# RWKV stage: the recurrence's 128-row output products of all chunks ahead of its 64-row chain, and the low-rank decay and rate as stacked fp32r products

## The chip, the cores and the metric

The kernel runs on one core of a Trainium2 chip. The metric is the device time of one execution in microseconds (us). TensorE is the matrix engine (PE in the rows, PEld its weight loads), DVE the vector engine, ACT the scalar engine, POOL GpSimd, SP the queue that issues the DMAs. fp32r is a 32-bit float format that TensorE multiplies in one pass and with fewer bits than fp32; a product is brought back near fp32 by splitting an operand into a high and a low part.

## The reference, cut to what matters

The program computes a first block (a hybrid of convolution and state-space layer) and a second block of two layers on 512 positions of width 1024. In the second block a layer is a feed-forward part, a mixer and another feed-forward part. The even layer's mixer joins a short convolution and an RWKV recurrence of 8 heads with 64 channels. This is the part that the change touches:

```python
r, k, v, dw, da, dg = jnp.split(p_rwkv, _RWKV_SPLITS, axis=-1)   # dw, da: 32 columns each, dg: 96
log_w = -jax.nn.softplus(-(w0 + jnp.tanh(dw) @ w_up)) - 0.5
decay = jnp.exp(-jnp.exp(log_w))
a = jax.nn.sigmoid(a0 + da @ a_up)
...
def step(S, inp):
    r_t, w_t, k_t, v_t, a_t, b_t = inp
    Sa = jnp.einsum('bhvk,bhk->bhv', S, a_t)
    S = S * w_t[:, :, None, :] + Sa[..., None] * b_t[:, :, None, :] + v_t[..., None] * k_t[:, :, None, :]
    return S, jnp.einsum('bhvk,bhk->bhv', S, r_t)
```

The output is then normalized by head, gated and projected together with the convolution's output.

## The kernel before, in words

Activations lie transposed: channels on the 128 partitions, the 512 positions along the free axis. Weights are streamed by SP's queue (`wload`, L234), split into a high part by a cast on ACT (L235) and a low part by a subtraction (L236, on POOL in this stage, on DVE elsewhere), and each 128x128 block is multiplied in three fp32r matmuls of 512 columns (L247, L248, L249). Split activations are made by a cast on ACT (L253) and a subtraction on DVE (L254).

The RWKV stage is the function `even`. Its 8 heads are worked on in two halves of four heads; a half is two pairs of heads (`jj` = 0, 1), and the two heads of a pair share the 128 partitions. The 512 positions are cut into 8 chunks of 64. For each half these steps follow each other:

- `lora` (once): the columns of dw and da come out of the input projection in a tile `la`: rows 0 to 31 for the decay, 32 to 63 for the rate. L1147 takes the Tanh of the first 32. `inproj` projects and shifts k, r and v.
- `prep_half`: decay and rate for 128 channels at a time by fp32 products with 32 rows (L1194, L1198) of `la` with the weights `wau`, then a scan of the logarithms of the decay and exponentials, on ACT, DVE and POOL.
- `quads` (L1249): products of all pairs of positions in a chunk, masked on DVE (L1253). A part goes out to memory (`nd`) and comes back in another layout, `subst` inverts small triangles on DVE, the result goes out (`td`) and comes back (`b<-td`).
- `wmats` (L1309 to L1336) completes the inverses of the 64x64 triangles by small products; `uvmats` (L1350, L1356) transposes; `premats` (L1381 to L1406) makes for each chunk a transition matrix and an added term, in two groups of four chunks (`g` = 0, 1), and the tile `u_`, whose lower 64 rows come out of this step.
- `chain_half`: for each chunk `cc` and each pair of heads the state is carried on by two products of 64 rows (L1438), an fp32 matmul being two instructions in the trace, and an addition on DVE into the next state; the chunk's output is a product of 128 rows that needs no state (L1445, 64 output channels of one head) and, from the second chunk on, one of 64 rows on the state (L1448). Both add up in a bank of PSUM for each pair of heads (`yb`). At the end ACT copies the banks out (L1457).
- `post_half` normalizes (sums by L1471 and L1475, root and reciprocal L1477 and L1478, spread by L1482) and gates (L1489); `outp` projects.

The first half's chain stands in the program after the second half's `quads` and `subst`; the convolution (`conv_in`, `conv_out`) and the first half's output are work without a place in this order. A planner in the framework sorts all instructions by the priorities of EV_PRIO and its own simulated times, engine by engine, and puts in the waits; each engine then runs its list in order. Buffers of 128x512 come from a first-in, first-out list `S` of 27; a buffer that was given back comes to the end of it. `tc.issue_after(x)` makes the instructions of its block stand behind x on their engine.

The chain's loop before:

```python
ps = yb[jj][:, 64 * cc:64 * cc + 64]
for h, sl in enumerate(hs):
    MM(ps[sl], u_[:, 128 * c4 + 64 * h:128 * c4 + 64 * h + 64], d["qt"][jj, h, g][0][:, c4, 64:128],
       start=True, stop=cc == 0)
    if cc:
        MM(ps[sl], state(jj, cc)[sl], a4[sl, cc, 1], start=False, stop=True)
```

Of the kernel before, what the change touches and what calls it, by code (L numbers as in the profile page):

```python
# [8 lines left out]
F32 = mybir.dt.float32  # L9
R = mybir.dt.float32r  # L10
AF = mybir.ActivationFunctionType
ALU = mybir.AluOpType
PSUM = bass.MemoryType.PSUM
T = 512
# [26 lines left out]
def pack(inp):  # L41
    f = {}
    a = {k: np.asarray(v) for k, v in inp.items()}
# [34 lines left out]
    mu = np.zeros((14, 128), np.float32)  # L78
    mus = a["even_mu_shift_2"][0]
    mu[:12] = mus[:1536].reshape(12, 128)  # L80
    mu[12, :64], mu[13, :96] = mus[1536:1600], mus[1600:]
    put("mu", mu.T)
    for n, src in (("w0", "rwkv_w0_2"), ("a0", "rwkv_a0_2"), ("k_k", "rwkv_k_k_2"), ("k_a", "rwkv_k_a_2"),
                   ("r_k", "rwkv_r_k_2"), ("gn_w", "rwkv_ln_w_2"), ("gn_b", "rwkv_ln_b_2")):
# [19 lines left out]
    for k in range(8):  # L104
        for g in range(2):
# [17 lines left out]
    ew = a["even_w_in_2"][0]  # L123
    wpad = np.zeros((1024, 26 * 128), np.float32)
    wpad[:, :3072] = ew[:, :3072]
    wpad[:, 3072:3136], wpad[:, 3200:3296] = ew[:, 3072:3136], ew[:, 3136:3232]
    cb, rr, kk, vv = 0, 12, 16, 20
    f["even_in"] = pairs(wpad, [(24, 25), (kk, kk + 1), (rr, rr + 1), (vv, vv + 1), (kk + 2, kk + 3),
                                (rr + 2, rr + 3), (vv + 2, vv + 3)]
                         + [(4, 8), (5, 9), (0, 1), (6, 10), (7, 11), (2, 3)])  # L130
    f["lora"] = np.concatenate([a["rwkv_w_up_2"][0], a["rwkv_a_up_2"][0]], 0)
    f["g_up"] = a["rwkv_g_up_2"][0]
    wo = a["even_w_out_2"][0].reshape(8, 128, 8, 128)

# [914 lines left out]
def even(P, nxt):  # L1049
# [8 lines left out]
    with ExitStack() as ctx:  # L1058
# [5 lines left out]
        def c(name, shape, dt=F32):  # L1064
            return ph0.tile(list(shape), dt, name=name)
# [4 lines left out]
        TS(out=half[:, 12:16], in0=half[:, 8:12], scalar1=-1.0, scalar2=1.0, op0=ALU.mult, op1=ALU.add)  # L1070
        hw0, ha0, hka, oka = (lambda j, b=b: half[:, 4 * b + j:4 * b + j + 1] for b in range(4))
        wn = c("wn", (96, 512))
        wau, nr = wn[0:64], wn[64:96]
        nc.sync.dma_start(wau, ap["lora"])
        gup = c("gup", (96, 512))
        nc.sync.dma_start(gup, ap["g_up"])
        bones = c("bones", (128, 128))
# [47 lines left out]
        def proj(i, kind="mm"):  # L1125
            h, l = P.wload(ap["even_in"][i], 2048)
            out = []
            for a in range(2):
                ps = P.bank(kind)
                P.mm3(ps, h, l, 1024 * a, P.xh, P.xl)  # L1130
                out.append(ps)
            return out
# [6 lines left out]
            STT(out=out, in0=out, scalar=P.v("mu", mi), in1=pt[:, 1:], op0=ALU.mult, op1=ALU.add)  # L1139
            return out  # L1140

        la, lg = S.get(), S.get()

        def lora():
            pa, pb = proj(0)
            shifted(pa, 12, la)
            A.activation(la[0:32], la[0:32], AF.Tanh)  # L1147
            shifted(pb, 13, lg)
            A.activation(lg, lg, AF.Tanh, scale=0.5)
            TS(out=lg, in0=lg, scalar1=0.5, scalar2=0.5, op0=ALU.mult, op1=ALU.add)  # L1150
# [22 lines left out]
        def prep_half(hf, tmp, kind):  # L1173
            d = D_[hf]
            k_, r_, v_, kkr, ar, bk, pc, bv = (d[n] for n in ("k", "r", "v", "kkr", "ar", "bk", "pc", "bv"))
            X = Slots(tmp)
            pss = P.bank(kind)
            for jj in range(2):
                j = 2 * hf + jj
                kkr[jj] = S.get()  # L1180
                TS(out=kkr[jj], in0=k_[jj], scalar1=P.v("k_k", j), scalar2=None, op0=ALU.mult)
                sq = X.get()
                A.activation(sq, kkr[jj], AF.Square)
                MM(pss[64:96], sel[:, jj, :], sq, start=jj == 0, stop=jj == 1)
                X.put(sq)
            TS(out=nr, in0=pss[64:96], scalar1=1e-24, scalar2=None, op0=ALU.max)
            A.activation(nr, nr, AF.Sqrt)
            V.reciprocal(nr, nr)

            def stages(jj):  # L1190
                j = 2 * hf + jj
                js = slice(128 * j, 128 * j + 128)
                ps = P.bank(kind)
                MM(ps, wau[0:32, js], la[0:32], start=True, stop=True)  # L1194
                ld, L = X.get(), X.get()
                A.activation(ld, ps, AF.Tanh, scale=0.5, bias=hw0(j))
                ps = P.bank(kind)
                MM(ps, wau[32:64, js], la[32:64], start=True, stop=True)  # L1198
                ta, av = X.get(), X.get()
                A.activation(ta, ps, AF.Tanh, scale=0.5, bias=ha0(j))  # L1200
                TS(out=ld, in0=ld, scalar1=1.0, scalar2=DECAY_C, op0=ALU.add, op1=ALU.mult)
                V.tensor_tensor_scan(out=L, data0=rst, data1=ld, initial=0.0, op0=ALU.mult, op1=ALU.add)
                GP.tensor_tensor(out=ld, in0=L, in1=ld, op=ALU.subtract)
                TS(out=av, in0=ta, scalar1=0.5, scalar2=0.5, op0=ALU.mult, op1=ALU.add)
                TS(out=ta, in0=ta, scalar1=hka(j), scalar2=oka(j), op0=ALU.mult, op1=ALU.add)
                yield
                e2 = X.get()
                A.activation(e2, L, AF.Exp)
                A.activation(L, L, AF.Exp, scale=-1.0)
                A.activation(ld, ld, AF.Exp)  # L1210
                e3 = L
                V.tensor_copy(pc[jj], ch(e2)[:, :, 63])
                kh = ta
                TT(out=kh, in0=ta, in1=k_[jj], op=ALU.mult)
                S.put(k_[jj])
                pk = P.bank(kind)
                MM(pk, selT[:, jj, :], nr, start=True, stop=True)
                TT(out=kkr[jj], in0=kkr[jj], in1=pk, op=ALU.mult)
                yield
                ar[jj], bk[jj] = B.get(), B.get()  # L1220
                a4, b4 = (x.rearrange("p (c a t) -> p c a t", a=2, t=64) for x in (ar[jj], bk[jj]))
                STT(out=a4[:, :, 0], in0=ch(kkr[jj]), scalar=-1.0, in1=ch(ld), op0=ALU.mult, op1=ALU.mult)
                TT(out=a4[:, :, 1], in0=ch(r_[jj]), in1=ch(e2), op=ALU.mult)
                TT(out=av, in0=av, in1=kkr[jj], op=ALU.mult)
                S.put(kkr[jj])
                TT(out=b4[:, :, 1], in0=ch(av), in1=ch(e3), op=ALU.mult)
                TT(out=b4[:, :, 0], in0=ch(kh), in1=ch(e3), op=ALU.mult)
                X.put(ld, e2, e3, av)
                yield
                STT(out=r_[jj], in0=r_[jj], scalar=P.v("r_k", j), in1=kh, op0=ALU.mult, op1=ALU.mult)  # L1230
                X.put(ta)
                pb_ = P.bank(kind)
                MM(pb_, bones, r_[jj], start=True, stop=True)
                S.put(r_[jj])
                bv[jj] = S.free.pop() if hf else S.get()
                TT(out=bv[jj], in0=pb_, in1=v_[jj], op=ALU.mult)

            return stages
# [177 lines left out]
        def chain_half(hf):  # L1416
            d = D_[hf]
            cb = P.bank("ch")
            yb = [P.bank("ch") for _ in range(2)]
            sg = [S.get() for _ in range(2)]  # L1420
            hs = [slice(64 * h, 64 * h + 64) for h in range(2)]

            def mc(jj, cc):
                m, o = d["mc"][jj, cc // 4], 64 * (cc % 4)
                return m[:, o:o + 64], m[:, 256 + o:320 + o]

            def state(jj, cc):
                return mc(jj, 0)[1] if cc == 1 else sg[jj][:, 64 * cc:64 * cc + 64]

            for cc in range(8):  # L1430
                g, c4 = cc // 4, cc % 4
                for jj in range(2):
                    if 0 < cc < 7:
                        m, c_ = mc(jj, cc)
                        s0 = state(jj, cc)
                        ps = cb[:, 256 * jj + 64 * (cc % 4):256 * jj + 64 * (cc % 4) + 64]
                        for sl in hs:
                            MM(ps[sl], m[sl], s0[sl], start=True, stop=True)  # L1438
                        TT(out=state(jj, cc + 1), in0=ps, in1=c_, op=ALU.add)
                for jj in range(2):  # L1440
                    a4 = d["ar"][jj].rearrange("p (c a t) -> p c a t", a=2, t=64)
                    u_ = d["uv"][jj, g]
                    ps = yb[jj][:, 64 * cc:64 * cc + 64]
                    for h, sl in enumerate(hs):
                        MM(ps[sl], u_[:, 128 * c4 + 64 * h:128 * c4 + 64 * h + 64], d["qt"][jj, h, g][0][:, c4, 64:128],  # L1445
                           start=True, stop=cc == 0)
                        if cc:
                            MM(ps[sl], state(jj, cc)[sl], a4[sl, cc, 1], start=False, stop=True)  # L1448
                if c4 == 3:
                    for jj in range(2):  # L1450
                        if not hf:
                            S.put(d["qt"][jj, 0, g][1], d["qt"][jj, 1, g][1])
                            if jj:
                                S.put(d["uv"][jj, g])
            for jj in range(2):
                d["yo"][jj] = S.get()
                A.copy(d["yo"][jj], yb[jj])  # L1457
                B.put(d["ar"][jj], d["wt"][jj][1])
                S.put(sg[jj])
                if not hf:  # L1460
                    S.put(d["mc"][jj, 0], d["mc"][jj, 1])
# [550 lines left out]
```

## Time and profile before

| | |
|---|---|
| median of 3 runs | 2668.18 us (2662.55 to 2675.57) |
| profiled execution | 2676.43 us, of which the span from the first to the last instruction is 2674.7 us |
| mean granted TensorE clock | 0.962 |
| the stage `even` | about 947 to 1350 us of the span |
| the two chains | 1172.5 to 1310 us of the span, woven into other work |

A span's rows tell when an engine was busy, by line of the kernel. Matmuls are pipelined, so the time that one costs is the distance from its start to the next one's, not its duration. The granted clock is given as a share of full speed.

### The profile page before, as it was taken

The numbers are of one execution on the slowest core, as the hardware profiler recorded it, in microseconds if no ns is written. First come the engines' busy times: TensorE is split into PE (matmuls) and PEld (weight loads), VectorE is DVE, ScalarE is ACT, GpSimd is POOL, SyncE is SP. The second block draws the span as 40 slices with busy tenths as digits, with TensorE's granted clock in tenths as the row PEclk, the third lists the DMA queues.
The fourth block names the chain that finished last, engine by engine and source line by source line (L and its number), as shares of the span: only waits on it lengthen the run. The fifth ranks groups of instructions, "written<-read, shape, count | busy, mean of one in ns | idle before, by whom it ended". The sixth has DMA issues, their size and how long they took to land.

```text
span 2674.7 us, 31936 instructions
## 1 busy us (share of the span) xinstructions
PE 2550.5 (95%) x12732; PEld 2075.1 (78%) x12732; DVE 1466.0 (55%) x1970; ACT 921.8 (34%) x1316; POOL 485.4 (18%) x331
## 2 busy tenths in 40 slices
PE   8687899999999999999999999999999988999999
PEld 7565788888888876778578888888888767788887
DVE  7889868455344468543564344443444776643442
ACT  5254436243223333221143223422223565422221
POOL 2499602020000164321010000100001231100000
PEclk9798999999999999898799999999999989999999
DMA  4222332323232432224122322322324422123323
GB/s 169 83 81 73 94 107 94 130 71 99 89 108 90 127 114 63 58 58 113 40 87 85 104 99 86 106 95 91 106 90 131 117 74 71 63 95 92 106 90 100
DMA packets 116230, 250.81 MB, mean 94 GB/s; under 512 B 44112, under 2 KB 53072, under 8 KB 116080
## 3 DMA queue, kind: packets, MB, share of 16 engines
q1 hardware_dynamic: 115936, 248.54, 29.7%
q8 instruction: 100, 1.64, 0.3%
q14 instruction: 50, 0.41, 0.1%
q10 hardware_dynamic: 144, 0.22, 0.0%
HBM read 234.16 MB, written 13.37 MB: 93 GB/s over the span
## 4 chain that ended last, share of the span: by engine, by line
PE 79%; DVE 9%; POOL 3%; issue 2%; ACT 2%; DMA 1%; SPq 0%; DVEq 0%; ACTq 0%; POOLq 0%
PE bank L247 24%; PE bank L248 24%; PE bank L249 23%; POOL xa L764 1%; DVE wl L236 1%; DVE xa L769 1%; PE bank L1887 1%; POOL acc L264 1%; PE bank L1445 0%; PE bank L1249 0%; DMA b<-td 0%; PE bank L1448 0%; ACT wh L235 0%; DMA s<-nd 0%; PE bank L1312 0%
## 5 line engine op out<-in xcount | busy, mean ns | idle before, releaser
L247 PE MATMUL bank<-xh,wh 128*128 128x512 f32 (+1 forms) x2152 | 841.5, 393 | 16.1 <-ACT xh L976 5.8
L235 ACT CAST wh<-raw 128x1024 fp32r<-128x1024 f32 x448 | 432.9, 967 | 1225.0 <-PE bank L248 918.0
L248 PE MATMUL bank<-xl,wh 128*128 128x512 f32 (+1 forms) x2152 | 842.3, 392 | 3.5 <-DVE xl L946 2.4
L249 PE MATMUL bank<-xh,wl 128*128 128x512 f32 (+1 forms) x2152 | 840.9, 392 | 0.2 <-DVE wl L236 0.2
L236 DVE TENSOR_TENSOR wl<-raw,wh 128x1024 fp32r<-128x1024 f32 (+2 forms) x414 | 480.5, 1161 | 327.4 <-ACT wh L235 324.8
L247 PEld LDWEIGHTS bank<-xh,wh 128*128 128x128 f32 x2152 | 409.5, 191 | 107.0 <-ACT xh L976 6.4
L248 PEld LDWEIGHTS bank<-xl,wh 128*128 128x128 f32 x2152 | 411.0, 191 | 91.7 <-DVE xl L977 4.1
L249 PEld LDWEIGHTS bank<-xh,wl 128*128 128x128 f32 x2152 | 411.0, 191 | 89.5 <-issue 5.5
L264 POOL TENSOR_TENSOR acc<-acc,sq 128x512 f32<-128x512 f32 x54 | 90.1, 1669 | 1303.9 <-ACT sq L263 1297.3
L248 PE MATMUL bank<-ml,wh 128*128 128x512 f32 x704 | 273.9, 389 | 0.0
L249 PE MATMUL bank<-mh,wl 128*128 128x512 f32 x704 | 273.9, 389 | 0.0
L247 PE MATMUL bank<-mh,wh 128*128 128x512 f32 x704 | 272.6, 389 | 0.0
L331 DVE TENSOR_TENSOR up<-bank,rs 128x512 f32<-128x512 f32 x88 | 60.8, 691 | 271.2 <-PE bank L249 271.2
L327 DVE TENSOR_TENSOR gp<-bank,rs 128x512 f32<-128x512 f32 x88 | 60.8, 691 | 174.3 <-PE bank L249 174.1
L248 PEld LDWEIGHTS bank<-ml,wh 128*128 128x128 f32 x704 | 132.2, 188 | 27.4
L247 PEld LDWEIGHTS bank<-mh,wh 128*128 128x128 f32 x704 | 132.2, 188 | 27.4
L249 PEld LDWEIGHTS bank<-mh,wl 128*128 128x128 f32 x704 | 132.2, 188 | 27.4
L236 POOL TENSOR_TENSOR wl<-raw,wh 128x1024 fp32r<-128x1024 f32 x34 | 85.5, 2515 | 176.1 <-ACT wh L235 140.6
L764 POOL TENSOR_TENSOR xa<-xa,cw 128x512 f32<-128x512 f32 x60 | 101.4, 1691 | 10.3 <-ACT cw L763 7.6
L339 DVE SCALAR_TENSOR_TENSOR xa<-bank,xa 128x512 f32<-128x512 f32 x64 | 44.3, 691 | 79.4 <-PE bank L249 79.4
L253 ACT CAST mh<-m 128x512 fp32r<-128x512 f32 x88 | 55.0, 626 | 58.7 <-DVE m L333 58.7
L742 PE MATMUL bank<-cph,wh 128*128 128x256 f32 x128 | 39.4, 308 | 32.2 <-ACT cph L725 32.2
(643 smaller groups left out, 2962.9 us busy)
## 6 DMA issues: line engine op xcount, KB each, us to landing
raw<-in_ffn_gu_dram SPq DMA_DIRECT2D x176, 512.0 KB, 3.5
raw<-in_ffn_dn_dram SPq DMA_DIRECT2D x64, 512.0 KB, 3.5
raw<-in_w_in_dram SPq DMA_DIRECT2D x46, 512.0 KB, 3.5
raw<-in_even_in_dram SPq DMA_DIRECT2D x26, 512.0 KB, 3.6
raw<-in_ffn_dn_dram SPq DMA_DIRECT2D x64, 192.0 KB, 2.3
raw<-in_conv_dram SPq DMA_DIRECT2D x16, 512.0 KB, 3.8
xa<-in_xT_dram SPq DMA_DIRECT2D x16, 256.0 KB, 4.1
raw<-in_w_co_dram SPq DMA_DIRECT2D x8, 512.0 KB, 3.4
```

Source lines behind the costliest of these rows:

```text
L235: nc.scalar.copy(h[:, :m], raw[:, :m])
L236: self.wlo.tensor_tensor(out=l[:, :m], in0=raw[:, :m], in1=h[:, :m].bitcast(F32), op=ALU.subtract)
L247: self.nc.tensor.matmul(ps, h[i][:, s], xh[k], start=a, stop=False)
L248: self.nc.tensor.matmul(ps, h[i][:, s], xl[k], start=False, stop=False)
L249: last = self.nc.tensor.matmul(ps, l[i][:, s], xh[k], start=False, stop=b)
L253: self.nc.scalar.copy(hi, src)
L264: nc.gpsimd.tensor_tensor(out=acc, in0=acc, in1=sq, op=ALU.add)
L327: nc.vector.tensor_tensor(out=gp, in0=pg, in1=rs, op=ALU.mult)
L331: nc.vector.tensor_tensor(out=up, in0=pu, in1=rs, op=ALU.mult)
L339: nc.vector.scalar_tensor_tensor(out=P.x[o], in0=ps, scalar=0.5, in1=P.x[o], op0=ALU.mult, op1=ALU.add)
L742: nc.tensor.matmul(d, h[:, o], xh, start=a, stop=False)
L764: GP.tensor_tensor(out=y, in0=y, in1=w, op=ALU.add)
```

## The change

The 128-row products of all 8 chunks are issued in a block of their own ahead of the chain, for each pair of heads and head the 8 chunks one after another; the first of each eight starts the accumulation in its half of the bank, and the others are issued behind it. The chain's loop keeps the products on the state. In `lora` the columns of dw and da are laid out twice each (rows 0 to 63 the decay's, 64 to 127 the rate's), by the packed weights; the rows of the first copy are kept as the fp32r high part, those of the second become the low part. The up-projection's weights are loaded as 128 rows (twice each), split into high and low, and a product is two fp32r matmuls of 64 rows instead of one fp32 matmul of 32. The load of these weights moves from the set-up into `lora`, and the tile `la` is given back after it.

```diff
-    mu[12, :64], mu[13, :96] = mus[1536:1600], mus[1600:]
+    mu[12], mu[13, :96] = np.concatenate([mus[1536:1568]] * 2 + [mus[1568:1600]] * 2), mus[1600:]
...
-    wpad[:, 3072:3136], wpad[:, 3200:3296] = ew[:, 3072:3136], ew[:, 3136:3232]
+    wpad[:, 3072:3200] = np.concatenate([ew[:, 3072:3104]] * 2 + [ew[:, 3104:3136]] * 2, 1)
+    wpad[:, 3200:3296] = ew[:, 3136:3232]
...
-    f["lora"] = np.concatenate([a["rwkv_w_up_2"][0], a["rwkv_a_up_2"][0]], 0)
+    f["lora"] = np.concatenate([a["rwkv_w_up_2"][0]] * 2 + [a["rwkv_a_up_2"][0]] * 2, 0)
...
-        wau, nr = wn[0:64], wn[64:96]
-        nc.sync.dma_start(wau, ap["lora"])
+        nr = wn[64:96]
+        wuh, wul, lx = c("wuh", (128, 512), R), c("wul", (128, 512), R), c("lx", (128, T), R)
...
-        la, lg = S.get(), S.get()
+        lg = S.get()
 
         def lora():
+            raw = S.get()
+            nc.sync.dma_start(raw, ap["lora"])
+            P.split(raw, wuh, wul)
+            S.put(raw)
             pa, pb = proj(0)
+            la = S.get()
             shifted(pa, 12, la)
-            A.activation(la[0:32], la[0:32], AF.Tanh)
+            A.activation(la[0:64], la[0:64], AF.Tanh)
+            A.copy(lx, la)
+            for o in (32, 96):
+                TT(out=lx[o:o + 32], in0=la[o:o + 32], in1=lx[o:o + 32].bitcast(F32), op=ALU.subtract)
+            S.put(la)
...
-                MM(ps, wau[0:32, js], la[0:32], start=True, stop=True)
+                for n, w in enumerate((wuh, wul)):
+                    MM(ps, w[0:64, js], lx[0:64], start=n == 0, stop=n == 1)
...
-                MM(ps, wau[32:64, js], la[32:64], start=True, stop=True)
+                for n, w in enumerate((wuh, wul)):
+                    MM(ps, w[64:128, js], lx[64:128], start=n == 0, stop=n == 1)
...
+            first = None
+            for jj in range(2):
+                for h, sl in enumerate(hs):
+                    for cc in range(8):
+                        with tc.issue_after(first.ins) if cc else ExitStack():
+                            m = MM(yb[jj][sl, 64 * cc:64 * cc + 64], d["uv"][jj, cc // 4][:, 128 * (cc % 4) + 64 * h:128 * (cc % 4) + 64 * h + 64],
+                                   d["qt"][jj, h, cc // 4][0][:, cc % 4, 64:128], start=cc == 0, stop=False)
+                        first = first if cc else m
             for cc in range(8):
...
-                    u_ = d["uv"][jj, g]
-                    ps = yb[jj][:, 64 * cc:64 * cc + 64]
-                    for h, sl in enumerate(hs):
-                        MM(ps[sl], u_[:, 128 * c4 + 64 * h:128 * c4 + 64 * h + 64], d["qt"][jj, h, g][0][:, c4, 64:128],
-                           start=True, stop=cc == 0)
+                    for sl in hs:
                         if cc:
-                            MM(ps[sl], state(jj, cc)[sl], a4[sl, cc, 1], start=False, stop=True)
+                            MM(yb[jj][sl, 64 * cc:64 * cc + 64], state(jj, cc)[sl], a4[sl, cc, 1], start=False, stop=cc == 7)
```

## Rows read from the trace of the kernel before

**Rows 1.** The page: busy time in us (share of the span) xinstructions of each engine.

```profile
PE 2550.5 (95%) x12732; PEld 2075.1 (78%) x12732; DVE 1466.0 (55%) x1970; ACT 921.8 (34%) x1316; POOL 485.4 (18%) x331
```

**Rows 2.** Busy time by stretches: length, engines (xinstructions), granted clock, DMA share, GB/s.

```profile
940.00:985.00 45.00, 45.00 (x198) 36.88 (x197) 30.41 (x39) 13.99 (x15) 30.46 (x28) 1.00 0.41 135
985.00:1100.00 115.00, 105.98 (x467) 75.56 (x466) 95.35 (x123) 37.01 (x50) 56.02 (x29) 0.91 0.28 71
...
1172.00:1196.40 24.40, 20.48 (x139) 16.44 (x138) 8.37 (x16) 5.78 (x9) 8.51 (x4) 0.96 0.24 54
1196.40:1217.50 21.10, 20.94 (x115) 15.52 (x115) 8.73 (x22) 3.78 (x5) 5.64 (x2) 0.88 0.69 155
1217.50:1250.00 32.50, 31.67 (x309) 26.75 (x310) 12.92 (x25) 2.92 (x5) 3.35 (x2) 0.63 0.38 115
1250.00:1290.00 40.00, 40.00 (x626) 32.54 (x625) 13.27 (x27) 11.40 (x23) 3.40 (x2) 1.00 0.20 61
1290.00:1312.00 22.00, 20.14 (x83) 11.01 (x81) 10.62 (x16) 3.09 (x5) 0.00 (x0) 0.58 0.09 25
```

**Rows 3.** TensorE in order of time: start, us, line, out<-in, tile. One full-clock step.

```profile
1210.24 0.33 PE L1438 MATMUL bank<-s,s 64*64 64x64 f32 x4
1210.41 0.28 PE L1448 MATMUL bank<-b,s 64*64 64x64 f32 x2
1210.61 0.33 PE L1445 MATMUL bank<-s,s 128*64 128x64 f32 x2
1210.87 0.33 PE L1448 MATMUL bank<-b,s 64*64 64x64 f32 x2
1211.13 0.33 PE L1445 MATMUL bank<-s,s 128*64 128x64 f32 x2
1211.38 0.50 PE L247 MATMUL bank<-cr,wh 128*128 128x512 f32 x1
```

**Rows 4.** The chain of waits (start, us, what): runs of 16 of one shape.

```profile
1264.70 0.93 PE bank L1390 x16
...
1267.56 0.61 PE bank L1401 x16
```

**Rows 5.** TensorE in order of time: a step at half clock, first and next.

```profile
1296.84 0.48 PE L1438 MATMUL bank<-s,s 64*64 64x64 f32 x4
...
1298.67 2.07 PE L1482 MATMUL bank<-wn,selT 32*128 32x512 f32 x2
```

**Rows 6.** Stretches, L1445 alone: length, matmul and weight-load busy (xinstructions), clock, DMA.

```profile
1172.00:1196.40 24.40, 2.44 (x24) 1.61 (x24) 0.96 0.24 54
1196.40:1217.50 21.10, 3.29 (x20) 1.91 (x20) 0.88 0.69 155
1217.50:1250.00 32.50, 4.16 (x20) 2.48 (x20) 0.63 0.38 115
1250.00:1290.00 40.00, 6.06 (x44) 3.68 (x44) 1.00 0.20 61
1290.00:1312.00 22.00, 4.15 (x20) 2.48 (x20) 0.58 0.09 25
```

**Rows 7.** The chain of waits around the second half's inverses and normalization.

```profile
1210.82 6.65 DMA b<-td
...
1250.52 0.23 PE bank L248
...
1291.44 3.36 DVE wn L1478
```

**Rows 8.** The low-rank tile's Tanh, its product, a split's subtraction (min/median/max), a DMA's issue.

```profile
959.69 0.63 ACT L1147 ACTIVATE s<-s 32x512 f32<-32x512 f32 x1
L1194 PE MATMUL bank<-s,wn x8: 587/587/692, 989.0 to 1050.5; 32*128 32x512 f32 x8
L254 DVE TENSOR_TENSOR ml<-m,mh x88: 682/685/693, 612.1 to 2613.6; 128x512 fp32r<-128x512 f32 x88
951.86 0.56 SPq L1074 DMA_DIRECT2D wn<-in_lora_dram  x1
```

## The prediction

> **What bounds the kernel now.** I read the page's head first, for the span, then the busy table by stretches, then the order of TensorE's instructions inside the recurrence, and last the chain of waits there. TensorE is busy 2550.5 us, 95% of the span [rows 1], so what counts is TensorE's time, and idle time of the others only where TensorE waits for them. The recurrence's output lies in 1172 to 1312 us. There the table has five stretches that I call A (1172 to 1196.4), B (to 1217.5), C (to 1250), M (to 1290) and D (to 1312) [rows 2]. TensorE is busy 20.5 of 24.4 us in A, 20.9 of 21.1 in B, 31.7 of 32.5 in C, all of M, and 20.1 of 22 in D. But busy is not dense. One step of one pair of heads reads: four L1438 (64x64 tiles) at 1210.24, two L1448 (64x64) at 1210.41, two L1445 (128x64) at 1210.61, two L1448 at 1210.87, two L1445 at 1211.13, the next matmul at 1211.38 [rows 3]. That is 1.14 us for ten short instructions. A run of 16 that keeps one tile takes 0.93 us of the chain, 0.058 each [rows 4]. The two L1445 between L1448 take 0.26 us, and the two L1448 between L1445 0.26 us, against 0.12 for two of a run: every change of tile shape costs about 0.14 us. At the half clock (1.2 of 2.4 GHz) a step takes 1298.67 - 1296.84 = 1.83 us [rows 5].
>
> **Part 1, the chain.** The diff moves the 128-row products (L1445) out of the steps. Nothing is added or removed: 128 instructions stay, and no DMA moves. After it a step is four L1438 and four L1448 of one shape. The first four take 0.17 us [rows 3]; I price the other four alike, and 0.09 us for the change at the end (estimated: each step now has one such change where it had four): 0.43 us. A step saves 1.14 - 0.43 = 0.71 us, or 0.355 for each pair of L1445 taken out. At half clock I put 0.27 + 0.27 + 0.14 = 0.68 against 1.83: 0.57 a pair. Against this stand the products in runs. No row shows a long run of one 128x64 tile; the nearest is the one-tile 64x64 run, 0.058 each [rows 4], so one half's 64 take 3.7 us, 4.0 with the changes at its ends. Bounds: 0.038, as 16 of L1401, 128x64 on two tiles in turn, take 0.61 us with the change at the end [rows 4], and 0.13, half a lone pair's 0.26 [rows 3].
>
> Now by stretch, with the counts of L1445 [rows 6] (two to a pair; the four pairs of chunk 0 in each half already run together):
> - A, 12 pairs, 8 of them in steps: 8 x 0.355 = 2.8 us saved, 0.5 of chunk 0 goes into the run, 4.0 paid: 0.7 us lost. It lies on the path, since the second half's masks (L1249) stand behind it, and they feed a DMA out and back that ends in the load of td at 1217.5 [rows 7].
> - B, 10 pairs: 3.5 us of TensorE. I book nothing. TensorE stands waiting for that load and the DVE copy behind it at the end of B, so what gets done earlier meets the same wait. Bounds 0 and 3.5, the latter if later products fill the room.
> - C, 10 pairs, 6 of them at half clock by the pace of their steps: 6 x 0.57 + 4 x 0.355 = 4.8 us. TensorE is nearly always busy, so most of it is path; some will turn into waits for the DVE copies between the inverse's steps. I take 4, bounds 2 and 4.8.
> - M, 22 pairs, 18 in steps: 6.4 + 0.5 saved, 4.0 paid, 2.9 us. Here the steps are already woven into other 64x64 work, which saves them changes now; I take 1.3, bounds 0 and 2.9.
> - D, 10 pairs, again 6 at half clock: 3.4 + 1.4 us. The 1.4 comes ahead of the reciprocal L1478, 3.36 us from 1291.44, for whose end at 1294.8 TensorE stands waiting [rows 7]; it turns into a longer wait. 3.4 counts, as the chain's end releases the second half's normalization and the last output product. Bounds 2 and 4.8.
> The sum is -0.7 + 0 + 4 + 1.3 + 3.4 = 8.0 us saved; the ends are some 3 and 18 (all upper bounds, and 1.3 more in each half if the runs go at 0.038).
>
> A new order is added: in a bank, every output product on a state (L1448) now comes behind all eight products of its half bank, and those of chunks 4 to 7 need the second group's U. In the second half this holds back up to 24 L1448 of chunks 1 to 3 from about 1270 to after 1283. Behind them waits only the copy of the bank at the very end; the recurrence itself (L1438) writes another bank. TensorE has other work in M, so this is a shift and I book nothing; uncovered it would be 24 x 0.042 = 1.0 us in D.
>
> **A rule that speaks against this.** The one-tile runs above go at 0.058 us an instruction at full clock, each with its own weights [rows 4]. The Trainium skill, TensorE: Matmul & The Clock Gate, section Part 3 (Packing small matmuls — row/col tiling), says that a weight load overlaps a matmul in flight only where their row groups differ. By that rule the products of one head, all on the same rows, would go at load plus matmul. The 64x64 runs, which share their rows too, don't bear it out, so it gets a small chance as a rival below.
>
> **Part 2, the low-rank products.** Removed: 16 fp32 instructions of 32 rows (L1194 and L1198, 0.587 us each, two at a time on different rows) [rows 8]. Added: 16 fp32r ones of 64 rows. Two at a time the old ones take at most 8 x 0.587 = 4.7 us. The new ones, at 0.23 us, the step of the long products [rows 7], take 3.7 us one after another and 1.8 two at a time. So 0 to 2.9 us of TensorE, the low end likelier, since 0.587 holds the pipeline's tail and 0.23 doesn't. But in 985 to 1100 DVE is busy 95.4 of 115 us and TensorE 106 [rows 2]; the path runs through DVE, so I book 0. Added to the preparation: a cast and a copy on ACT (some 0.6 us each), on DVE a 128x512 subtraction (0.685 us, as L254) and two of 32x512 that I put at 0.7 each: 2.1 us of DVE. They are covered: the Tanh of this tile runs at 959.69 and its first reader at 989.0 [rows 8], and DVE is busy only 30.4 of 45 us in 940 to 985. Without cover it is 2.1 + 0.7 us. The load, twice as large, moves from the set-up into this place on SP's queue, behind the clears of td and ahead of or between the weight loads; TensorE is busy 45 of 45 us there [rows 2], so a weight tile that comes late costs directly; I bound it by the issue of one DMA, 0.56 us [rows 8]. Freeing one buffer shifts all later ones by one; I book 0. Part 2: 0, between 2.9 us saved and 2.8 + 0.6 = 3.4 lost.
>
> **The sum.** The profiled execution took 2676.4 us (span 2674.7 and 1.7 around it); less 8, 2668.4. That execution is 8.2 us above the median of the three runs, 2668.2, and the saving is the same there: **2660 us**, 0.3% faster.
>
> **The rivals.** (a) *The clock recovers.* C and D run at 0.63 and 0.58 of the clock [rows 2], so some 18 us of D are at half. TensorE fell into both after a stretch of steps with shape changes and a wait. If denser work keeps one of them up, 18 us of half-clock work takes 18 x 1.14/1.83 = 11, so 7 us more and the full 4.8 of C: 2651. For it speaks that M, also of small tiles but dense, runs at 1.00; against it that the waits for td and for L1478 remain, or grow. (b) *The clock falls more*: the side of slower. With 128-row work gone from the steps, and waits grown by 3.5 us ahead of 1217.5 and 1.4 ahead of 1294.84, the chain becomes short bursts between waits, and TensorE falls to half in A, B or M too. An 18 us stretch of full-clock work then takes 18 x 1.83/1.14 = 29, 11 us more. One such stretch decides: 2660 + 11 = 2671, above before. Against: M is full at 1.00. (c) *The saving isn't there*: if C's and D's gain turns into waits for DVE as well, since every step passes through a DVE addition, only 1 or 2 us are left: 2667. (d) *Slow runs of one tile*, the rule above: at 0.13 the products cost 64 x 0.072 = 4.6 us more in A and in M, both on the path: 2669.
>
> **How the numbers follow.** Forecast 0.52 (2660, its own range 2652 to 2668), (a) 0.17, (b) 0.13, (c) 0.12, (d) 0.06. The 80% range goes from 2644 (2668 less the 18 of the chain's upper end and 6 of (a)) to 2677 ((b)'s 2671, less the 3 of the sum's lower end for its 8, so 2676, and a part of what the tile can lose). A measurement tells about 0.5%, 13.3 us, from no change. Faster by more: (a) mostly and the forecast's lower edge, 0.27. Slower by more: the outer part of (b) and a shifted order of work, 0.09. Within: 0.64.
>
> **What would show it.** The timeline of TensorE should show L1445 as runs of 16, at 0.058 each, ahead of the second half's masks and in M; steps of L1438 and L1448 with no 128x64 between them, near 0.43 us at full clock; the load of td landing no earlier; a longer wait ahead of L1482; and the chain's last L1448 some 8 us earlier. L1445 at 0.13 would be (d); granted clock in C and D tells (a) from (b). What would make it wrong: another order of the whole stage, since the planner weighs all instructions anew, or the low-rank tile coming late at 989.

## The result, and the profile after

The changed kernel takes 2651.3 us (median of 7, 2650.8 to 2656.5), the kernel before 2671.7 us (median of 7). The ratio is 0.9925, 95% interval 0.9909 to 0.9941: 20 us faster, where 8 were forecast from 2668 to 2660. Measured again beside the experiments it was 0.9924 (0.9898 to 0.9950). So the direction and the 80% range (2644 to 2677) held, 2651.3 lies just outside the forecast's own range (2652 to 2668), and the forecast saving was less than half of what came.

Line numbers in the changed kernel: the products are L1447, the recurrence L1458, the products on a state L1464, the reciprocal L1494 and its spreading L1498; the long products are L248 to L250, and the first instruction of the second half's `wmats` is L1324.

The page of the changed kernel, span and busy time, against [rows 1]:

```profile
span 2649.1 us, 31928 instructions
...
PE 2524.1 (95%) x12732; PEld 2057.5 (78%) x12732; DVE 1461.4 (55%) x1973; ACT 921.9 (35%) x1318; POOL 481.4 (18%) x331
```

The profiled execution took 2650.8 us, so it stands for the median. TensorE runs the same 12732 matmuls and is busy 26 us less; that is the whole difference of the spans. All of it lies in this stage, from about 947 us to 1363 before and to 1338 after.

To compare stretches of two kernels I cut them at events, not at times: the stage's beginning, the chain's first step (which begins A and B), the first product of `wmats` for the second half (C), the first transpose of its `premats` (M), its sums of squares in the first half's normalization (D), the last product of the second chain. Busy time by these stretches (columns as in [rows 2]), first of the kernel before:

```profile
947.10:1172.50 225.40, 216.38 (x1449) 165.09 (x1447) 151.23 (x200) 64.77 (x91) 101.17 (x66) 0.93 0.25 72
1172.50:1218.30 45.80, 40.92 (x252) 31.67 (x251) 17.34 (x38) 9.56 (x14) 14.15 (x6) 0.93 0.45 102
1218.30:1258.90 40.60, 40.57 (x425) 33.29 (x426) 14.26 (x27) 6.48 (x13) 6.75 (x4) 0.71 0.32 102
1258.90:1288.80 29.90, 29.90 (x508) 25.65 (x506) 10.78 (x23) 7.22 (x14) 0.00 (x0) 1.00 0.22 64
1288.80:1309.80 21.00, 19.14 (x82) 9.98 (x80) 11.04 (x17) 3.12 (x5) 0.00 (x0) 0.61 0.10 26
```

and of the changed one:

```profile
947.80:1168.70 220.90, 211.83 (x1447) 161.63 (x1446) 147.99 (x202) 66.80 (x94) 101.64 (x67) 0.95 0.26 76
1168.70:1209.00 40.30, 36.93 (x306) 29.13 (x304) 17.99 (x42) 9.10 (x14) 11.19 (x5) 1.00 0.47 108
1209.00:1242.00 33.00, 32.34 (x377) 27.79 (x378) 13.28 (x24) 5.24 (x12) 6.78 (x4) 0.69 0.41 124
1242.00:1269.80 27.80, 27.80 (x528) 24.96 (x527) 10.87 (x24) 6.89 (x14) 0.00 (x0) 1.00 0.27 80
1269.80:1286.90 17.10, 13.62 (x59) 5.90 (x60) 11.05 (x17) 3.87 (x6) 0.00 (x0) 0.64 0.04 14
```

The first number after the times is the length: 4.5 us are won ahead of the chain, 5.5 in A and B, 7.6 in C, 2.1 in M, 3.9 in D, and 2 in the rest behind. The seventh number is the granted clock. The stretches of two kernels do not hold the same work (A and B hold 252 matmuls before and 306 after), so their lengths tell where the time went and not what one edit cost or saved there.

The load of td, with which B ends, landed at 1208.2 us, 9.3 us sooner than before [rows 7], though the chain's first step came only 3.8 us sooner (start, time, what):

```profile
1203.45 4.70 DMA b<-td
```

The chain's own shape came out as priced. The chain of waits of the changed kernel (start, time, engine, output, line, count) shows the first half's products:

```profile
1173.51 3.34 PE bank L1447 x64
```

TensorE in order of time (start, duration of one, instruction, count, and the wait in brackets) shows a step at full clock, the wait for the reciprocal, and a step at half clock:

```profile
1190.18 0.33 PE L1458 MATMUL bank<-s,s 64*64 64x64 f32 x4
1190.35 0.28 PE L1464 MATMUL bank<-b,s 64*64 64x64 f32 x4
1190.56 0.66 PE L1362 MATMUL bank<-ident,b 128*128 128x128 f32 x4
...
1275.82 2.07 PE L1498 MATMUL bank<-wn,selT 32*128 32x512 f32 x2 [3.04 <-DVE wn L1494]
...
1280.67 0.48 PE L1458 MATMUL bank<-s,s 64*64 64x64 f32 x4
1280.94 0.42 PE L1464 MATMUL bank<-b,s 64*64 64x64 f32 x4
1281.30 2.07 PE L1505 MATMUL bank<-s,gup 96*128 96x512 f32 x2
```

64 products take 3.34 us, 0.052 each; a step takes 0.38 us at full clock (1190.18 to 1190.56) and 0.63 at half, against 1.14 and 1.83 [rows 3, 5].

### The profile page after: what moved, and what is told of

It is laid out like the page before. It is cut to its first block, busy times and chain, and to the rows that moved or that the text cites. A ratio compares the mean times of both kernels' runs of the same rounds, so it can differ in the third digit from the quotient of the medians.

```text
span 2649.1 us, 31928 instructions
## 1 busy us (share of the span) xinstructions
PE 2524.1 (95%) x12732; PEld 2057.5 (78%) x12732; DVE 1461.4 (55%) x1973; ACT 921.9 (35%) x1318; POOL 481.4 (18%) x331
## 4 chain that ended last, share of the span: by engine, by line
PE 79%; DVE 9%; POOL 3%; issue 2%; ACT 2%; DMA 1%; SPq 0%; DVEq 0%; ACTq 0%; POOLq 0%
PE bank L248 24%; PE bank L249 24%; PE bank L250 24%; POOL xa L765 1%; DVE wl L237 1%; PE bank L1903 1%; DVE xa L770 1%; POOL acc L265 1%; PE bank L1337 0%; PE bank L1261 0%; ACT wh L236 0%; DVE xl L271 0%; DMA b<-td 0%; PE bank L1324 0%; PE bank L1397 0%
## 5 line engine op out<-in xcount | busy, mean ns | idle before, releaser
L248 PE MATMUL bank<-xh,wh 128*128 128x512 f32 (+1 forms) x2152 | 837.4, 391 | 13.0 <-ACT xh L977 5.8
L250 PE MATMUL bank<-xh,wl 128*128 128x512 f32 (+1 forms) x2152 | 837.5, 390 | 2.7 <-DVE wl L237 2.7
L248 PEld LDWEIGHTS bank<-xh,wh 128*128 128x128 f32 x2152 | 407.2, 190 | 104.3 <-issue 6.4
L250 PEld LDWEIGHTS bank<-xh,wl 128*128 128x128 f32 x2152 | 408.7, 190 | 87.2 <-DVE wl L237 3.6
L250 PE MATMUL bank<-mh,wl 128*128 128x512 f32 x704 | 273.9, 389 | 0.0
L248 PE MATMUL bank<-mh,wh 128*128 128x512 f32 x704 | 272.6, 389 | 0.0
L250 PEld LDWEIGHTS bank<-mh,wl 128*128 128x128 f32 x704 | 132.1, 188 | 27.5
L248 PEld LDWEIGHTS bank<-mh,wh 128*128 128x128 f32 x704 | 132.1, 188 | 27.4
L743 PE MATMUL bank<-cph,wh 128*128 128x256 f32 x128 | 40.6, 317 | 32.3 <-ACT cph L726 32.3
```

The costliest lines, as they stand in the source:

```text
L248: self.nc.tensor.matmul(ps, h[i][:, s], xh[k], start=a, stop=False)
L250: last = self.nc.tensor.matmul(ps, l[i][:, s], xh[k], start=False, stop=b)
L743: nc.tensor.matmul(d, h[:, o], xh, start=a, stop=False)
```

## The experiments

The kernels before and changed are compared in single profiles, but the runs of one and the same kernel spread. The 55 runs of the kernel before that stand beside the experiments, on three chips, go from 2662.7 to 2681.1 us, and each comes with its mean granted clock, from 0.962 to 0.970. A straight line through them has a slope of -2.3 us for 0.001 of clock, with a correlation of -0.88; at 0.964 the mean is 2678.6 us, at 0.967 2670.0, at 0.970 2664.9. The three chips' runs lie on it alike, within 0.3 us in the mean. By estimate, 0.001 of the mean clock over 2672 us is 5.3 us at half clock, and a step, which takes 1.14 us at full clock and 1.83 at half [rows 3, 5], loses 0.38 of such a time, so 2.0 us: the slope has the size that the clock alone would give. So I put each kernel's runs against that line: the mean distance from it at the run's own clock is the difference at equal clock (a single run lies some 3 us off the line, so a mean is good to 1 or 2 us), and what the kernel's mean clock is worth on the line is the clock's part. Both are estimates: they take it that the clock is worth the same in every kernel, and a kernel that sheds work done at half clock raises its mean clock by that alone.

| kernel | runs | median us | ratio to before (95%) | mean clock | at equal clock, us | clock's part, us |
|---|---|---|---|---|---|---|
| changed | 7 | 2651.3 | 0.9925 (0.9909 to 0.9941) | 0.9674 | -17 | -3 |
| changed, again | 6 | 2653.0 | 0.9924 (0.9898 to 0.9950) | 0.9683 | -15 | -5 |
| chain alone | 9 | 2659.0 | 0.9949 (0.9931 to 0.9968) | 0.9689 | -7 | -7 |
| low-rank alone | 12 | 2671.6 | 0.9999 (0.9978 to 1.0021) | 0.9627 | -6 | +8 |
| products by chunk | 12 | 2661.1 | 0.9962 (0.9948 to 0.9977) | 0.9669 | -9 | -2 |
| buffer alone | 12 | 2664.9 | 0.9970 (0.9952 to 0.9988) | 0.9679 | -2 | -4 |
| chain and buffer | 6 | 2658.4 | 0.9945 (0.9925 to 0.9965) | 0.9690 | -8 | -7 |
| changed, list as before | 6 | 2655.5 | 0.9936 (0.9915 to 0.9958) | 0.9670 | -15 | -2 |
| heads in turn | 6 | 2650.8 | 0.9915 (0.9895 to 0.9935) | 0.9680 | -18 | -5 |
| heads in turn, again | 6 | 2650.4 | 0.9915 (0.9892 to 0.9938) | 0.9670 | -21 | -2 |
| most products left out | 5 | 2656.1 | 0.9937 (0.9916 to 0.9959) | 0.9644 | -20 | +4 |
| wait filled | 6 | 2655.6 | 0.9939 (0.9918 to 0.9959) | 0.9668 | -15 | -2 |
| low-rank back in fp32 | 6 | 2644.9 | 0.9899 (0.9879 to 0.9918) | 0.9715 | -15 | -13 |

### Each part alone

The chain's edit alone and the low-rank edit alone; the diffs are the two parts of the change.

> Only the chain's edit, the low-rank part as before. If the gain is TensorE's time freed by fewer changes of tile shape (theory S), nearly all of it stands: 15 to 20 us under before, ratio 0.9925 to 0.9945, and the stretch from the second half's masks to the load of td is shorter already. If a good part came from the low-rank edit or from the buffers that it shifts (theory B), 6 to 10 us, ratio 0.996 to 0.998.

Measured: 0.9949, 14 us faster. That is just short of what theory S expected (15 to 20) and beyond theory B's 6 to 10: most of the gain, not nearly all. In its profile, by the same events:

```profile
1173.20:1218.70 45.50, 37.48 (x281) 29.75 (x280) 20.23 (x39) 9.56 (x14) 13.29 (x6) 0.96 0.42 98
1218.70:1253.50 34.80, 34.44 (x399) 28.09 (x400) 14.78 (x27) 6.92 (x14) 6.71 (x4) 0.80 0.47 128
1253.50:1280.40 26.90, 26.90 (x526) 24.62 (x524) 10.09 (x22) 5.88 (x12) 0.00 (x0) 1.00 0.26 79
1280.40:1296.60 16.20, 12.72 (x60) 5.75 (x60) 11.04 (x17) 3.90 (x6) 0.00 (x0) 0.72 0.05 13
```

A and B are 0.3 us shorter though TensorE is busy 3.4 us less in them: the time turned into waiting. The waits of TensorE in this kernel:

```profile
PE bank L247 <- DVE c L1525: 4.0, 1, 4.0
PE bank L1486 <- DVE wn L1482: 3.0, 1, 3.0
PE bank L1312 <- DVE xl L1309: 2.9, 1, 2.9
```

The third is the wait for the load of td and the copy behind it; before, TensorE stood 0.9 us there. The second is the wait for the reciprocal, 1.9 before. The load of td landed at 1217.8 us, 44.6 behind the chain's first step, against 45.0 before: the 3.4 us saved ahead of it hardly brought it forward, against the last clause of theory S.

> Only the low-rank edit, the chain as before. Theory S: no difference, within 3 us of before (ratio 0.999 to 1.001). Theory B: 8 to 14 us faster (ratio 0.995 to 0.997), with the second half's masks done some 4 us earlier as in the changed kernel.

Measured: 0.9999, as theory S expected. But its profile is the slowest of all, and shows what hides behind a median of no difference. M of this kernel:

```profile
1252.80:1303.40 50.60, 50.60 (x508) 43.53 (x505) 10.09 (x22) 7.77 (x14) 0.00 (x0) 0.50 0.08 24
```

These are the same 508 matmuls that took 29.9 us at 1.00 in the kernel before; here all of them run at 0.50. Over its 12 runs the low-rank edit alone is 6 us better at equal clock and loses 8 to a lower clock. Two of the runs, the profiled one among them, are at 0.955 and 0.953, below all that the line was drawn through; without them the loss is 4 us.

### Half the shape changes

```diff
 for jj in range(2):
-    ...
     for h, sl in enumerate(hs):
-        MM(ps[sl], u_[...], d["qt"][...], start=True, stop=cc == 0)
-        if cc:
-            MM(ps[sl], state(jj, cc)[sl], a4[sl, cc, 1], start=False, stop=True)
+        MM(yb[jj][sl, ...], u_[...], d["qt"][...], start=cc == 0, stop=False)
+for jj in range(2):
+    for sl in hs:
+        if cc:
+            MM(yb[jj][sl, ...], state(jj, cc)[sl], a4[sl, cc, 1], start=False, stop=cc == 7)
```

> Kernel before, with the 128-row products kept in each chunk's step but put together: the four products of both pairs of heads, then the four on the state. About half of the shape changes go (four in a chunk and pair become two), no product moves ahead of the chain. Theory S: about half of the chain's gain, 7 to 11 us (ratio 0.996 to 0.9975). If it is the place ahead of the chain that counts and not the changes of shape (theory P), within 3 us of before.

Measured: 0.9962, 10 us. It is what theory S expected, and with no product ahead of the chain theory P falls. The next experiment shows that another order alone can bring nearly as much at the median, so what speaks for the grouping by shape is TensorE's own time. In the traces the stage has 257 changes of tile shape on TensorE before, 205 here, 183 with the chain's edit; start to start, without the waits, chain and products cost 34.1, 20.9 and 19.1 us of TensorE, at the clock of each profile. So 52 of the 74 changes that the chain's edit removes brought 13 of its 15 us.

### Is it the buffers, or the arithmetic of the low-rank part?

```diff
-        la, lg = S.get(), S.get()
+        la, lg = c("la", (128, T)), S.get()
```

> Kernel before with one edit: the low-rank tile has a buffer of its own, so that all buffers taken later from the list shift by one as in the changed kernel; no work changes. Theory S: within 3 us of before. Theory B in its form that the buffers' shift is the cause: 5 us or more faster.

Measured: 0.9970 (0.9952 to 0.9988), 8 us faster with not one instruction of work changed: outside what theory S allowed. At equal clock it is 2 us, so this gain is for the most part another order of the same work meeting the clock otherwise. That led to theory L.

> The chain's edit alone, with the low-rank tile in a buffer of its own so that the list of buffers is one longer, and the low-rank products as before. In the traces the chain's edit alone did 11 us less TensorE work but waited 5 us more, and the buffer alone did the same work with 12 us less lost to the half clock. Theory L (the list of buffers is what the low-rank edit brings): all of the changed kernel's gain, 18 to 22 us under before, ratio 0.992 to 0.9935. Rival A (the arithmetic of the low-rank products brings it): as the chain's edit alone, 0.9949.

> The changed kernel, but the low-rank tile keeps its buffer as before and the weights' staging has one of its own, so that the list of buffers is that of before. Theory L: as the chain's edit alone, ratio 0.994 to 0.996, with TensorE waiting some 4 us near 1192 again. Rival A: as the changed kernel, 0.9925.

The first is the chain's edit with the one line above, the second the changed kernel with `la` kept and a staging tile outside the list:

```diff
-        lg = S.get()
+        la, lg = S.get(), S.get()
+        raw = c("rawl", (128, T))
...
```

Measured: 0.9945 with the buffer added to the chain's edit, no different from 0.9949 without; 0.9936 for the changed kernel with the old list, nearer to the changed kernel than to the chain alone, and at equal clock the same 15 us. The intervals (0.9925 to 0.9965 and 0.9915 to 0.9958) reach into both theories' ranges, so the medians alone don't decide; at equal clock, 8 us for the one and 15 for the other, theory L falls on both. The wait near 1192 did not come back at 4 us either; it was 1.4.

> The changed kernel with the low-rank products again in fp32 with 32 rows, one instead of two; the larger load in its new place, the split and the stacked tile are still made, but not read. Theory N (the new products' price in the planner's simulated time moves the long products ahead of the chain: 562 of them instead of 549 stand ahead of its first step): the order falls back to that of the chain's edit alone, ratio 0.994 to 0.996. Rival M (moving the load and the preparation does it): the order and the time stay those of the changed kernel, 0.992 to 0.9935.

```diff
-                for n, w in enumerate((wuh, wul)):
-                    MM(ps, w[0:64, js], lx[0:64], start=n == 0, stop=n == 1)
+                MM(ps, raw[0:32, js], la[0:32], start=True, stop=True)
```

(and the same for the rate; raw and la in tiles of their own.) Measured: 0.9899, the fastest kernel of all, 8 us under the changed kernel on the same chip. The buffers differ too, as raw and la no longer come from the list. So the fp32r form of the low-rank products is not what gains beside the chain: theory N falls. Rival M is right in that the preparation in its new place is enough, but neither the order nor the time stayed those of the changed kernel: 521 long products stand ahead of the chain's first step, 562 in the changed one, 549 before, and that step comes at 1161.6 us, against 1168.7 and 1172.5. At equal clock it equals the changed kernel; by the line its 8 us are the clock, 0.9715.

### What the products still cost

> The changed kernel with the products of the two heads of a pair in turn instead of eight of one head after another. The work is the same. If two 128x64 tiles in turn run nearer to 0.03 us an instruction than the 0.052 of the runs now, the 128 products take some 2 to 3 us of TensorE less; of these half may reach the end: ratio to before 0.9915 to 0.9925, against 0.9925 for the changed kernel. If the planner's order changes with it, anything up to 5 us either way.

```diff
+                first = {}
-                for h, sl in enumerate(hs):
-                    for cc in range(8):
+                for cc in range(8):
+                    for h, sl in enumerate(hs):
...
```

> The products of a pair's two heads in turn, once more, on the same chip as the changed kernel. If the 3 us of TensorE that it saves reach the end, 2 to 4 us under the changed kernel (0.9985 to 0.9993 of it); if they are lost in the waits behind, or in the planner's other order, within 1.5 us of it.

Measured: 0.9915 twice. The first half's products in the chain of waits of the second of these:

```profile
1174.16 2.02 PE bank L1448 x64
```

0.032 us each with two tiles in turn, 0.052 with one, so 2.6 us less for both halves. On the same chip the medians are 2650.4 and 2653.0 us for the changed kernel, whose runs go from 2644.6 to 2658.2: the size fits, but it is not shown to be more than chance.

> The changed kernel without the 128-row products of chunks 1 to 7 (the output lacks their part): what the runs of products still cost. Theory S: their 112 instructions take 112 x 0.052 = 5.8 us of TensorE and no more, so 3 to 7 us under the changed kernel, ratio to before 0.990 to 0.9915. If much more goes (10 us and over), the products cost something beyond their own time, as by holding up the second half's masks.

112 of the 128 products are left out here. Measured: 0.9937, not faster at all, against the 0.990 to 0.9915 expected. At equal clock it is 20 us under before, 3 to 5 under the changed kernel, near the 5.8 us of TensorE that are gone; by the line the clock, 0.9644, took that back.

### What the wait does to the clock

```diff
...
+            if not hf:
+                pd = P.bank(kind)
+                with tc.issue_after(last.ins):
+                    for n in range(14):
+                        MM(pd, wuh[:, 0:128], lx, start=n == 0, stop=n == 13)
```

> The changed kernel once more, beside the next three on the same chip: 0.9925 of before, within 0.0015, and a granted clock of 0.967 to 0.968.

> The changed kernel with 14 long fp32r products whose result nobody reads, set behind the sums of the first half's normalization, where TensorE stands 3.0 us waiting for the reciprocal (1272.8 to 1275.8 us) and then runs 13.7 us at half clock. They take 14 x 0.23 = 3.2 us, so up to 1 us more than the wait. Theory C (the wait is what costs the clock): the half-clock stretch there goes or gets shorter, 3 to 5 us under the changed kernel in spite of the added work. Rival (the small tiles of the steps that follow cost it): the clock falls all the same, 0 to 3 us over the changed kernel.

Measured: the changed kernel 0.9924 again; with the wait filled 0.9939. In the trace of the filled one TensorE stands still for 0.55 us at most there, and the steps behind run at full clock up to 1286 us; first TensorE in order of time in the filled kernel, then the table of stretches for the wait and the steps behind it, once for the filled kernel and once for the unfilled one (two pieces, the wait and the steps):

```profile
1276.35 1.89 PE L1497 MATMUL bank<-lx,wuh 128*128 128x512 f32 x7
1278.17 0.33 PE L1458 MATMUL bank<-s,s 64*64 64x64 f32 x4
1278.43 1.89 PE L1497 MATMUL bank<-lx,wuh 128*128 128x512 f32 x7
1280.16 1.02 PE L1510 MATMUL bank<-s,gup 96*128 96x512 f32 x2
```

```profile
1275.00:1295.00 20.00, 18.90 (x89) 10.09 (x88) 12.80 (x21) 4.82 (x8) 0.00 (x0) 0.91 0.03 12
```

```profile
1274.00:1278.00 4.00, 0.90 (x17) 0.62 (x16) 3.40 (x2) 0.68 (x1) 0.00 (x0) 0.88 0.00 0
1278.00:1292.00 14.00, 13.62 (x47) 6.61 (x48) 7.91 (x16) 2.32 (x5) 0.00 (x0) 0.55 0.00 1
```

0.91 against 0.55 (over one and the same stretch, 1276.3 to 1290.5, it is 0.88 against 0.52): the wait is what costs the clock there, as theory C says, and D gets shorter in spite of 3.2 us of added work, 16.0 against 17.2 us. But the kernel did not: C was 36.7 us long in this profile and 34.4 in the other, the clock over the whole stage (945 to 1340) was 0.91 against 0.92, and the median is 2.6 us higher, where the rival put it. One pair of profiles shows the mechanism; the gain expected of it did not come.

## Why the prediction was right or wrong

**The price of a shape change, and of a step, right.** The products were forecast at 0.058 and run at 0.052; a step forecast at 0.43 and 0.68 us runs at 0.38 and 0.63. Part 1's price of 0.14 us a change carried the sum.

**Rival (d) did not happen.** One head's products run at 0.052 us an instruction, and a weight load of theirs lasts 0.13 to 0.14 (min, median, max in ns), so the weights are loaded beside the matmul before:

```profile
L1447 PEld LDWEIGHTS bank<-xa,xh x48: 132/138/138, 1249.6 to 1264.5; 128*64 128x64 f32 x48
```

The sentence of the Trainium skill, TensorE: Matmul & The Clock Gate, Part 3 (Packing small matmuls — row/col tiling), taken alone, does not hold for this run of 128x64 tiles on the same rows; the trace decides.

**The stretches.** These are cut at events, so the end of the prediction's C and the first 9 us of its M are one stretch here. With the chain's edit alone, A and B won 0.3 us (booked: 0.7 lost in A, nothing in B), and the saved time of B turned into the wait for td, 0.9 to 2.9 us. C won 5.8 (booked 4), M 3.0 (booked 1.3), D 4.8 (booked 3.4), and D's wait grew from 1.9 to 3.0 us as forecast. The sum is 13.9, booked 8.0. The difference goes with the clock: C went from 0.71 to 0.80 and D from 0.61 to 0.72, which is 2 x (0.29 x 40.6 - 0.20 x 34.8) = 9.6 and 2 x (0.39 x 21.0 - 0.28 x 16.2) = 7.3 us less at half clock, and at 1 - 1.14/1.83 = 0.38 for each of these us they are together worth 6.4 us. That is an upper end, since some of those us are work that the edit took out (the prediction has 12 pairs at half clock, 0.57 each, so 6.8 us). What is left is 7.5 or more, near the 8.0 booked and the 7 at equal clock.

In the changed kernel A and B won 5.5 us where 0.7 was booked as lost. The prediction let the saved time meet the same wait, and named "the load of td landing no earlier" as a sign; it holds with the chain's edit alone (1217.8 against 1217.5 us) and fails here (1208.2).

**Rival (a), its number without its sign.** The measured 2651.3 is the number of this rival (2651; its own terms, 7 and 0.8 off 2660, make 2652), but that is luck. Its sign was the granted clock in C and D, and these are at 0.69 and 0.64 in the changed kernel, against 0.71 and 0.61. What rose there is A and B, from 0.93 to 1.00. Something of it comes with the chain's edit alone, C at 0.80 and D at 0.72, and 7 us on the line over 9 runs; why the clock rises there is not shown. What I took as its proof is not certain either: M is at 1.00 in 13 of the 14 profiles, and at 0.50 in that of the low-rank kernel.

**Rival (b)** did not happen in the changed kernel, whose mean clock is 0.9674, against 0.9660 in the 55 runs before. The low-rank edit alone loses 8 us to the clock, but its steps are those of before and M has no wait in it, so this is not what the rival described. The kernel with most products left out comes nearest: 4 us on the line.

**Part 2, the term mis-sized.** Booked 0, between 2.9 saved and 3.4 lost. Alone its time is 0 (0.9999), 6 us better at equal clock and lost again to the clock. Beside the chain's edit it is 6 to 8 us at the medians and 8 to 10 at equal clock, outside those bounds. Its arithmetic was judged rightly: covered (the subtractions stand at 957 and 963 us and end by 965, the first reader starts at 972 and the next at 990), and back in fp32 nothing is lost. The step that failed is booking nothing for the new order of the stage that comes with this edit: I named the planner's new order as what would make the forecast wrong, and gave it no price. The shift of the buffers, for which I wrote "I book 0", is not it by itself: without the chain's edit it is 8 us at the median and 2 at equal clock, beside it nothing (0.9945 and 0.9949), and the changed kernel keeps its 15 us at equal clock with the old list. With the low-rank edit TensorE passes 562 long products ahead of the chain's first step, 13 more than before, and reaches it 3.8 us sooner; ahead of that step 11.7 us of the long products fall into half-clock stretches, 23.1 before (12.0 with the low-rank edit alone, 23.5 with the chain's alone); and the wait of 4.0 us near 1192 is 1.6. In A to C TensorE stands idle for 4.0 us, for 8.4 with the chain's edit alone.

**The sum.** 20 us at the median: some 7 of TensorE's work in the chain, near the 8 forecast, 3 to 5 of the clock, and 8 to 10 of another order of the stage that comes with the low-rank edit. This division goes by the line, and its last two parts overlap, since an order is worth what the clock does in it. Which piece of the low-rank edit's preparation moves the order (the load's place, the split, the stacked tile) stays open; the buffers' list and the form of the products are ruled out as its only causes.

**The chances.** Faster by over 0.5% had 0.27. With a price for the clock and for the order, each of them 5 to 8 us and as likely down as up, I would now put that chance near 0.4.

## What to carry to other kernels

Put matmuls of one tile shape together: here a change of shape costs 0.14 us, more than two of the small matmuls themselves, and regrouping inside a chunk already brings most of it. Before an engine's saved time is booked, look for the transfer or the slow instruction at which it waits next: with the chain's edit alone, the time saved ahead of the load of td and ahead of the reciprocal came back as waiting to within half a us. Ask as well whether the change moves that transfer: here it landed 9 us sooner in the changed kernel. In a kernel that a planner orders, test an edit beside one that shifts the order and does no work, and compare runs at equal clock: here such an edit is worth 8 us at the median and 2 at equal clock.

## What the runs showed of the hardware

The run-to-run spread of this kernel goes with TensorE's clock: 55 runs of one program follow it at -2.3 us for 0.001 (correlation -0.88). A dense stretch of small tiles is no guarantee of the full clock: the same 508 matmuls without a pause took 29.9 us at 1.00 in one kernel and 50.6 us at 0.50 in another, the only one of 14 profiles in which this stretch was not at full clock. And filling a wait of 3 us with matmuls that nobody reads lifted the clock of the steps behind it from 0.55 to 0.91; unfilled, about 14 us at half speed stood behind it. What was won there did not reach the end, as another stretch ran longer at half clock.
